# Split weights written to DRAM as two parts, and the router table's writes moved to ScalarE's DMA queue

## The chip, the cores and the metric

The kernel runs on one NeuronCore of a Trainium2 chip. The metric is device time in microseconds (us) of one launch. The kernel before took 3912.41 us (median of three runs, 3896.12 to 3922.23). TensorE (PE) does the matrix products, VectorE (DVE) and ScalarE (ACT) the elementwise work, GpSimd (POOL) issues the indirect gathers, and SyncE (SP) issues nearly all other transfers. SP and ACT each have a DMA queue of their own (q1 and q10 in the profile), POOL's is q0; all three are served by the same 16 DMA engines.

## What is computed

One layer of a hybrid encoder over 1024 prompt tokens and 8 x 16 sample tokens (9 blocks of 128 tokens, width 1024): a combined projection, chunk-band attention, an RG-LRU branch, a gated merge, then PEER (8 heads that each pick 16 of 16384 single-neuron experts).

```python
proj = jnp.einsum('btd,dc->btc', xn, w_in)             # 7 x 1024 columns
q, k, v, x_r, g_branch, gate_a, gate_r = jnp.split(proj, SPLITS, axis=-1)
merged = sigmoid(gate_a) * (o_attn @ w_ba) + sigmoid(gate_r) * (o_lru @ w_bl)
x = x + merged @ w_o
# PEER: s1, s2 = (xt @ wq) . keys; top_k; e_idx; g = softmax(top_s)
act = gelu(einsum('thkd,td->thk', expert_u[e_idx], xt))
out = einsum('thkd,thk->td', expert_v[e_idx], g * act)
```

## The kernel before

Blocks are worked in three groups of three: (0, 1, 8), (2, 3, 4), (5, 6, 7). For each group `mixer` runs five stages: LRU projections, gates and `w_bl`, attention (`w_in` columns for q, k, v and the gates), `w_ba` and `w_o`, and the `wq` projections with the scores. Every group needs the same 96 weight tiles of [128, 8, 128] f32 (512 KB): 56 of `w_in`, 8 each of `w_bl`, `w_ba` and `w_o`, 16 of `wq`. One tile is one projection: 24 matmuls over 384 columns, because each f32 weight w is split into a rounded part hi and a rest lo = w - hi, and `mm3` (L170 to L172) takes the three products hi·hi, hi·lo and lo·hi.

`load_split` makes the two parts. In group 0 it loads `raw` (L149, pool tag "raw", 4 buffers), casts it to hi on ACT (L136), subtracts on DVE (L137), and writes lo to DRAM (L165) for later. In groups 1 and 2 it loads `raw` again, casts it on ACT (L158) and loads lo from DRAM (L159). hi and lo stand in tags "hi" and "lo" of two buffers each, every third pair in `g_p` buffers. The "raw" tag is shared: in the `wq` stage of groups 0 and 1 the gains and the next group's x rows are loaded into it too.

Beside this, five blocks (`DENSE`) get their PEER output from dense products over all experts in a last stage (`dense`), and four (`GATHER`) by gathering rows. The first gather block is interleaved with groups 1 and 2; the others with `dense`. For `dense`, `build_g` makes a router table `G_d` in DRAM. It works through 20 pieces (5 blocks x 4): DVE makes one-hot tiles, PE multiplies them into PSUM tiles `pg` (L1013, L1014), ACT copies eight of these into one SBUF tile `st` (L1016), and `st` is written to `G_d` (L1018), 2 MB in runs of 256 bytes. `st` has one buffer, so the first copy of the next piece must wait until that write has landed. `fill`, `beat` and `tick` spread the pieces over the stages of groups 1 and 2; eight pieces fall into group 1, twelve into group 2.

PSUM tiles of the projections, `pg`, transposes and attention outputs share four buffers (tag "pp"); scores have two (tag "S"). Each engine takes its instructions strictly in the order that the scheduler wrote down; so does SP with its transfers.

Of the kernel before, what the change touches and what calls it, by code (L numbers as in the profile page):

```python
# [10 lines left out]
F32 = mybir.dt.float32  # L11
# [28 lines left out]
RAW_BUFS = 4  # L40
# [19 lines left out]
GCH = 2  # L60
# [5 lines left out]
def r32(ap):  # L66
    return ap.bitcast(F32R)
# [3 lines left out]
def kernel(ctx, tc, a):  # L71
    nc = tc.nc
    V, S, P, T = nc.vector, nc.scalar, nc.gpsimd, nc.tensor

    const = ctx.enter_context(tc.tile_pool(name="const", bufs=1))
    w_p = ctx.enter_context(tc.tile_pool(name="w", bufs=2))
# [5 lines left out]
    dr_p = ctx.enter_context(tc.tile_pool(name="dr", bufs=1, space=bass.MemoryType.DRAM))  # L82
# [52 lines left out]
    def split(hi, lo, src):  # L135
        S.copy(r32(hi), src)  # L136
        ins = V.tensor_tensor(r32(lo), src, hi, op=ALU.subtract)  # L137
        if phase[0] < 3:
            mark("V", ins)

    nw = [0]
    phase = [0, 0]

    lo_d = {}

    def load_split(src, hi=None, lo=None, shape=(128, KT, 128), raw=None, key=None):
        if raw is None:
            raw = w_p.tile(list(shape), F32, name="raw", tag="raw", bufs=RAW_BUFS)
            nc.sync.dma_start(raw, src)  # L149
        if hi is None and phase[0] in THIRD and nw[0] % 3 == 2:  # L150
            hi = g_p.tile(list(shape), F32, name="hi", tag="g3")
            lo = g_p.tile(list(shape), F32, name="lo", tag="g4")
        elif hi is None:
            hi = w_p.tile(list(shape), F32, name="hi", tag="hi")
            lo = w_p.tile(list(shape), F32, name="lo", tag="lo")
        nw[0] += 1
        if key in lo_d:
            S.copy(r32(hi), raw)  # L158
            nc.sync.dma_start(lo, lo_d[key])  # L159
            return hi, lo  # L160
        split(hi, lo, raw)
        if phase[0] == 0 and key:

            lo_d[key] = dr_p.tile(list(shape), F32, name="lo_%s%d" % key)
            nc.sync.dma_start(lo_d[key], lo)  # L165
        return hi, lo

    def mm3(out, l, r, first, last):
# [5 lines left out]
    def proj(src, x, Tn):  # L174

        hi, lo = load_split(a[src[0]][src[1]], key=src)
        ps = ps_p.tile([128, Tn], F32, name="pp", tag="pp")
        for k in range(KT):
            mm3(ps, (hi[:, k, :], lo[:, k, :]), (x[:, 0, k, 0:Tn], x[:, 1, k, 0:Tn]), k == 0, k == KT - 1)
        return ps  # L180
# [571 lines left out]
    def make_tables(b):  # L752
        if b in pending:
            pending.pop(b)()

    def table_parts(tab):
        h = tab.bitcast(F16)
        return h[:, 0:128], h[:, 128:256], tab[:, 128:192].bitcast(BF16), h[:, 384:512], h[:, 512:640]
# [213 lines left out]
    G_d = dr_p.tile([128, 128 // GCH, NCH, GCH, 32], F32, name="G_d")  # L972

    def build_g(gp, b):

        n0 = 4 * DENSE.index(b)
        st = {}

        def part(c, tb):
            def go():  # L980
                if c == 0 and tb == 0:
                    make_tables(b)
                    st["t"] = gp["st"].tile([128, 320], F32, name="tab")
                    nc.sync.dma_start(st["t"], tab_d[b])
                if tb == 0:
                    st["s"] = gp["st"].tile([128, 128, 32], F32, name="st")
                i1, i2, pw, hi, lo = table_parts(st["t"])
                sg = st["s"]
                t = c * 32 + tb * OH_T

                def row(x):
                    return x[:, t:t + OH_T].rearrange("p (g t) -> p g t", t=2).unsqueeze(2).to_broadcast(
                        [128, OH_T // 2, 128, 2])

                ow = gp["oh"].tile([128, OH_T // 2, 128, 2], BF16, name="ow")
                oh = gp["oh"].tile([128, OH_T // 2, 128, 2], F16, name="oh1")
                ol = gp["oh"].tile([128, OH_T // 2, 128, 2], F16, name="oh2")
                V.tensor_tensor(ow, gp["iota"], row(i2), op=ALU.is_equal)
                V.tensor_tensor(ow, ow, row(pw), op=ALU.mult)
                V.tensor_tensor(oh, gp["iota"], row(i1), op=ALU.is_equal)  # L1000
                V.tensor_tensor(ol, oh, row(lo), op=ALU.mult)
                V.tensor_tensor(oh, oh, row(hi), op=ALU.mult)
                later.append(lambda: products(c, tb, ow, oh, ol, sg))
                if len(later) > 1:
                    later.popleft()()
            return go

        def products(c, tb, ow, oh, ol, sg):
            for j0 in range(0, OH_T, 4):
                pg = ps_p.tile([128, 4, 128], F32, name="pg", tag="pp")  # L1010
                for j in range(4):
                    g, e = divmod(j0 + j, 2)
                    T.matmul(pg[:, j, :], ow[:, g, :, e], oh[:, g, :, e], start=True, stop=False)  # L1013
                    T.matmul(pg[:, j, :], ow[:, g, :, e], ol[:, g, :, e], start=False, stop=True)  # L1014
                t = tb * OH_T + j0
                S.activation(sg[:, :, t:t + 4].rearrange("p i t -> p t i"), pg, ACTF.Copy, scale=2.0 ** -13)  # L1016
            if tb == 32 // OH_T - 1:
                nc.sync.dma_start(G_d[:, :, n0 + c], sg.rearrange("p (a i) t -> p a i t", i=GCH))  # L1018

        later = deque()  # L1020
        return [part(c, tb) for c in range(4) for tb in range(32 // OH_T)] + [lambda: later.popleft()()]

    def dense(dp):
# [13 lines left out]
        def u_phase(e):  # L1037
            tick(2)
            hi, lo = load_split(a["peer_ut"][e], raw=u0 if e == 0 else None)
            wh = dp["w"].tile([128, Td], F32, name="wh")  # L1040
            wl = dp["w"].tile([128, Td], F32, name="wl")
            w = dp["w"].tile([128, Td], F32, name="wf", bufs=1)
            for m in range(0, Td, Td // 2):
                c1 = slice(m, m + Td // 2)
                ps = ps_p.tile([128, Td // 2], F32, name="pp", tag="pp")
                for k in range(KT):
                    mm3(ps, (hi[:, k, :], lo[:, k, :]), (xt2[:, 0, k, c1], xt2[:, 1, k, c1]), k == 0, k == KT - 1)
                S.activation(w[:, c1], ps, ACTF.Gelu_apprx_tanh)  # L1048
            w3 = w.rearrange("p (c t) -> p c t", t=32)
            V.tensor_tensor(w3, w3, router(e), op=ALU.mult)  # L1050
            split(wh, wl, w)
            return wh, wl

        def load_v(e):
            vh = dp["v"].tile([128, D], F32, name="vh")
            vl = dp["v"].tile([128, D], F32, name="vl")
            return load_split(a["peer_v"][e], vh, vl, (128, D))
# [254 lines left out]
```

## Time and profile before

| What | Value |
|---|---|
| median of 3 runs | 3912.41 us |
| the profiled execution's own time | 3894.32 us |
| its span in the trace | 3892.5 us |
| PE busy | 3629.8 us (93%) |
| DVE busy | 3049.4 us (78%) |
| ACT busy | 1624.7 us (42%) |
| DMA, mean of the span | 310 GB/s |
| group 0 | 0 to 620 us |
| groups 1 and 2 | 620 to 2055 us |
| dense stage | 2055 to 3892 us |

The page gives, for each engine, its busy time and share. A share over the whole span hides the stages, so the rows below are cut by stage. "Idle before <-" in a row names what ended the wait of that instruction, and a chain piece is a stretch of the path that ended last, followed back from the end.

### The profile page before, as it was taken

The page shows a single profiled execution, that of the slowest core. Times are in us where ns is not written, and L with a number is a line of the kernel's source. Part 1 is how long each engine was busy: PE and PEld are TensorE (multiplying, and loading weights), DVE is VectorE, ACT ScalarE, POOL GpSimd, SP SyncE. Part 2 cuts the span into 40 slices and gives each one's busy share as a digit, 9 for nine tenths or more (in the row PEclk, how much of TensorE's full clock was granted, in tenths as well). Part 3 has the DMA queues.
Part 4 walks back from the last instruction along what each step waited for, and adds up shares of the span by engine and source line. Part 5 has one row for each costly group of instructions (what it writes and reads, how often), then busy time and mean ns, then how long its engine had stood idle before and what let it go on. Part 6 is the DMA issues. An engine that isn't in the chain of part 4 may idle for free.

```text
span 3892.5 us, 59562 instructions
## 1 busy us (share of the span) xinstructions
PE 3629.8 (93%) x21775; PEld 3258.9 (84%) x21775; DVE 3049.4 (78%) x6332; ACT 1624.7 (42%) x2699; POOL 1429.2 (37%) x1094
## 2 busy tenths in 40 slices
PE   8998899899988889988788989999999999999998
PEld 7877799877778887777778878999999999999997
DVE  8433357968766588987669999998888998888997
ACT  7554346656644664666443222222222222222222
POOL 0000000123212012322210666665675665775662
PEclk9999999999999999999889999999999999999999
DMA  7778887888999889899996999898998998998995
GB/s 256 252 247 300 287 295 276 301 315 281 284 358 349 300 299 315 298 290 284 334 337 216 345 326 342 320 347 332 359 339 310 346 347 326 336 349 324 342 343 206
DMA packets 558423, 1208.05 MB, mean 310 GB/s; under 512 B 205361, under 2 KB 281521, under 8 KB 558129
## 3 DMA queue, kind: packets, MB, share of 16 engines
q1 hardware_dynamic: 380560, 638.23, 47.3%
q0 software_dynamic: 147456, 536.94, 38.4%
q10 hardware_dynamic: 30112, 29.09, 2.2%
q8 instruction: 170, 2.79, 0.3%
q14 instruction: 125, 1.02, 0.1%
HBM read 1066.15 MB, written 137.94 MB: 309 GB/s over the span
## 4 chain that ended last, share of the span: by engine, by line
PE 61%; DVE 13%; DMA 10%; ACT 6%; issue 3%; POOL 0%; ACTq 0%; SPq 0%; DVEq 0%; POOLq 0%
PE S L1085 19%; PE pp L170 12%; PE pp L171 12%; PE pp L172 12%; DMA G_d<-st 4%; DVE row L942 3%; PE S L529 2%; ACT st L1016 2%; DMA row<-peer_u,ei 1%; PE pt L458 1%; PE pp L543 1%; ACT hi L158 1%; DVE x L963 1%; DMA lo<-lo_w_in 1%; DVE lo L137 1%
## 5 line engine op out<-in xcount | busy, mean ns | idle before, releaser
L915 POOL DMA_INDIRECT row<-peer_u,ei x512 | 715.2, 1397 | 1172.0 <-DVE row L942 508.6
L915 POOL DMA_INDIRECT row<-peer_v,ei x512 | 687.8, 1343 | 793.4 <-DVE x L963 543.0
L963 DVE SCALAR_TENSOR_TENSOR x<-row,q,x 128x1024 f32<-128x1024 f32 x512 | 655.0, 1279 | 21.3 <-DMA row<-peer_v,ei 12.5
L170 PE MATMUL pp<-xd,hi 128*128 128x320 f32 x2048 | 635.9, 310 | 16.4 <-ACT wf L1048 12.8
L942 DVE SCALAR_TENSOR_TENSOR row<-row,xt 128x1024 f32<-128x1024 f32 x512 | 613.2, 1218 | 42.7 <-DMA row<-peer_u,ei 41.1
L172 PE MATMUL pp<-xd,lo 128*128 128x320 f32 x2048 | 634.3, 310 | 4.5 <-DVE lo L137 4.5
L171 PE MATMUL pp<-xd,hi 128*128 128x320 f32 x2048 | 634.7, 310 | 0.0
L170 PE MATMUL pp<-xn,hi 128*128 128x384 f32 x1344 | 480.2, 358 | 13.9 <-ACT hi L158 6.9
L171 PE MATMUL pp<-xn,hi 128*128 128x384 f32 x1344 | 463.2, 345 | 0.5 <-DVE xn L137 0.5
L172 PE MATMUL pp<-xn,lo 128*128 128x384 f32 x1344 | 461.1, 344 | 0.9 <-DMA lo<-lo_w_in 0.9
L136 ACT CAST hi<-raw 128x1024 fp32r<-128x1024 f32 x223 | 234.0, 1050 | 447.0 <-PE pp L171 329.6
L170 PEld LDWEIGHTS pp<-xd,hi 128*128 128x128 f32 x2048 | 386.8, 189 | 26.0 <-ACT wf L1048 15.6
L137 DVE TENSOR_TENSOR lo<-raw,hi 128x1024 fp32r<-128x1024 f32 x223 | 272.3, 1222 | 171.1 <-ACT hi L136 151.0
L1085 PE MATMUL S<-vh,wh 128*128 128x512 f32 x1280 | 397.2, 392 | 5.2 <-DVE acc L1093 3.5
L1085 PE MATMUL S<-vl,wh 128*128 128x512 f32 x1280 | 396.0, 390 | 1.7 <-DVE vl L137 1.7
L1085 PE MATMUL S<-vh,wl 128*128 128x512 f32 x1280 | 390.1, 394 | 5.9 <-DVE wl L137 5.9
L171 PEld LDWEIGHTS pp<-xd,hi 128*128 128x128 f32 x2048 | 386.7, 189 | 7.1
L172 PEld LDWEIGHTS pp<-xd,lo 128*128 128x128 f32 x2048 | 386.6, 189 | 6.6 <-DVE lo L137 4.8
L158 ACT CAST hi<-raw 128x1024 fp32r<-128x1024 f32 x192 | 200.5, 1047 | 316.3 <-PE pp L171 215.8
L1048 ACT ACTIVATE wf<-pp 128x320 f32<-128x320 f32 x256 | 106.7, 434 | 524.7 <-PE pp L172 316.8
L170 PEld LDWEIGHTS pp<-xn,hi 128*128 128x128 f32 x1344 | 261.7, 195 | 38.3 <-ACT hi L158 9.7
L1085 PEld LDWEIGHTS S<-vh,wl 128*128 128x128 f32 x1280 | 242.2, 190 | 58.3 <-DVE wl L137 7.8
(296 smaller groups left out, 6824.7 us busy)
## 6 DMA issues: line engine op xcount, KB each, us to landing
raw<-w_in SPq DMA_DIRECT2D x168, 512.0 KB
raw<-peer_v SPq DMA_DIRECT2D x128, 512.0 KB
raw<-peer_ut SPq DMA_DIRECT2D x127, 512.0 KB
lo<-lo_w_in SPq DMA_DIRECT2D x112, 512.0 KB
G_d<-st SPq DMA_DIRECT2D x20, 2048.0 KB
gt<-G_d SPq DMA_DIRECT2D x64, 640.0 KB
lo_w_in<-lo SPq DMA_DIRECT2D x56, 512.0 KB
raw<-wq SPq DMA_DIRECT2D x48, 512.0 KB
```

The lines of the kernel that those rows point to most:

```text
L136: S.copy(r32(hi), src)
L137: ins = V.tensor_tensor(r32(lo), src, hi, op=ALU.subtract)
L158: S.copy(r32(hi), raw)
L170: T.matmul(out, r32(lh), r32(rh), start=first, stop=False)
L171: T.matmul(out, r32(lh), r32(rl), start=False, stop=False)
L172: T.matmul(out, r32(ll), r32(rh), start=False, stop=last)
L529: T.matmul(s[:, m, 0:nh], st["q"][r0:r0 + 64, i * 128:(i + 1) * 128], kf[r0:r0 + 64, ko + m * nh:ko + (m + 1) * nh], start=True, stop=True)
L915: P.indirect_dma_start(out=t, out_offset=None, in_=table, in_offset=bass.IndirectOffsetOnAxis(ap=ei[:, j:j + 1], axis=0))
L942: V.scalar_tensor_tensor(u, u, 1.0, xt, op0=ALU.mult, op1=ALU.mult, accum_out=hh[:, j:j + 1])
L963: V.scalar_tensor_tensor(x2, v, q[:, j:j + 1], x2, op0=ALU.mult, op1=ALU.add)
L1048: S.activation(w[:, c1], ps, ACTF.Gelu_apprx_tanh)
L1085: T.matmul(po[:, m, :], r32(l[:, c1]), r32(r[:, m * 512:m * 512 + 512]), start=(n == 0 and q == 0 and (c == 0 or not held)), stop=(n == EC ...
```

## The change

Two things are changed. In group 0 the kernel writes hi as well as lo to DRAM (two transfers of 512 KB per tile, on SP's queue). In groups 1 and 2 it loads both parts and casts nothing: the raw load becomes the load of hi, and the ACT cast L158 is gone. The tiles change their tags in these groups: hi takes the four "raw" buffers and lo alternates between tags "lo" and "hi", four buffers in all. Second, the write of `st` to `G_d` is issued by ACT on its own queue in place of SP.

```diff
     def load_split(src, hi=None, lo=None, shape=(128, KT, 128), raw=None, key=None):
+        if key in lo_d:
+            nw[0] += 1
+            hi = w_p.tile(list(shape), F32, name="hi", tag="raw", bufs=RAW_BUFS)
+            lo = w_p.tile(list(shape), F32, name="lo", tag=("hi", "lo")[nw[0] % 2])
+            for t, d in zip((hi, lo), lo_d[key]):
+                nc.sync.dma_start(t, d)
+            return hi, lo
...
-        if key in lo_d:
-            S.copy(r32(hi), raw)
-            nc.sync.dma_start(lo, lo_d[key])
-            return hi, lo
         split(hi, lo, raw)
         if phase[0] == 0 and key:
-            lo_d[key] = dr_p.tile(list(shape), F32, name="lo_%s%d" % key)
-            nc.sync.dma_start(lo_d[key], lo)
+            lo_d[key] = [dr_p.tile(list(shape), F32, name="%s_%s%d" % (n, *key)) for n in ("hi", "lo")]
+            for t, d in zip((hi, lo), lo_d[key]):
+                nc.sync.dma_start(d, t)
...
-                nc.sync.dma_start(G_d[:, :, n0 + c], sg.rearrange("p (a i) t -> p a i t", i=GCH))
+                nc.scalar.dma_start(G_d[:, :, n0 + c], sg.rearrange("p (a i) t -> p a i t", i=GCH))
```

The scheduler writes a new order from it. Lines of the changed kernel lie five higher from L170 on. In group 0, SP's queue holds this before, near the start (cv and ck are the sample attention's cached values and keys):

```order
L165 DMA lo_w_in32_455<-lo_452 128x1024
L149 DMA raw_685<-w_in 128x1024
L165 DMA lo_w_in27_508<-lo_505 128x1024
L149 DMA raw_738<-w_in 128x1024
L165 DMA lo_w_in33_560<-lo_557 128x1024
```

and this in the changed kernel:

```order
L170 DMA hi_w_in32_461<-hi_457 128x1024
L170 DMA lo_w_in32_462<-lo_458 128x1024
L157 DMA raw_699<-w_in 128x1024
L170 DMA hi_w_in27_516<-hi_512 128x1024
L170 DMA lo_w_in27_517<-lo_513 128x1024
L157 DMA raw_754<-w_in 128x1024
L170 DMA hi_w_in33_570<-hi_566 128x1024
L170 DMA lo_w_in33_571<-lo_567 128x1024
```

One write per tile became two; everything behind them on SP moves back by one transfer per projection.

In the `wq` stage of group 2, ACT's order after the last copy of the second-last piece is, before (so is the score tile copied out, s_d its place in DRAM, pq a projection copied out of PSUM):

```order
L1016 ACTIVATE st_20313<-pg_20796 128x4x128
L729 COPY so_20883<-S_20876 128x768
L730 DMA s_d2_112<-so_20883 128x768
L158 CAST hi_20964<-raw_20962 128x1024
L719 COPY pq_20810<-pp_20752 128x384
L158 CAST hi_21050<-raw_21048 128x1024
L719 COPY pq_20874<-pp_20818 128x384
```

and in the changed kernel:

```order
L1021 ACTIVATE st_20143<-pg_20614 128x4x128
L1023 DMA G_d_135<-st_20143 8192x1x64
L734 COPY so_20699<-S_20692 128x768
L735 DMA s_d2_112<-so_20699 128x768
L724 COPY pq_20690<-pp_20634 128x384
L734 COPY so_20845<-S_20838 128x768
L735 DMA s_d2_112<-so_20845 128x768
L724 COPY pq_20774<-pp_20718 128x384
```

The casts are gone, and the write of the router piece stands two rows ahead of another transfer of ACT's own. Over the 20 pieces, ACT's next own transfer other than a router piece comes 1, 2, 2, 3, 3, 4, 5, 6, 9 and 13 rows behind in ten cases; in the other ten the next piece's write comes first, or 29 or more rows lie between.

In the `wq` stage of group 1, SP's order in the changed kernel is this (x and gain are the next group's rows and gain, in the same four "raw" buffers as hi):

```order
L153 DMA lo_12620<-lo_wq5_5932 128x1024
L153 DMA hi_12619<-hi_wq5_5931 128x1024
L153 DMA lo_12722<-lo_wq6_6047 128x1024
L223 DMA x_12698<-x 128x1024
L153 DMA lo_12784<-lo_wq7_6084 128x1024
L719 DMA keys_12555<-keysT 128x256
L230 DMA gain_12700<-norm_mix 128x1024
L153 DMA lo_12864<-lo_wq8_6177 128x1024
L719 DMA keys_12719<-keysT 128x256
L153 DMA hi_12721<-hi_wq6_6046 128x1024
```

Here hi of tile 6 comes after lo of tile 8: two of the "raw" buffers were given to x and gain first.

## Rows read from the trace of the kernel before

**Rows 1.** The page, part 4: the whole chain that ended last, by line.

```profile
PE S L1085 19%; PE pp L170 12%; PE pp L171 12%; PE pp L172 12%; DMA G_d<-st 4%; DVE row L942 3%; PE S L529 2%; ACT st L1016 2%; DMA row<-peer_u,ei 1%; PE pt L458 1%; PE pp L543 1%; ACT hi L158 1%; DVE x L963 1%; DMA lo<-lo_w_in 1%; DVE lo L137 1%
```

**Rows 2.** Windows by stage: busy time per engine, PE clock, DMA share, GB/s.

```profile
0.00:620.00 620.00, 558.35 (x3814) 503.80 (x3814) 303.43 (x755) 319.78 (x648) 26.27 (x70) 0.96 0.79 272
620.00:980.00 360.00, 339.96 (x1916) 293.55 (x1916) 296.97 (x1066) 219.23 (x390) 69.37 (x64) 0.96 0.83 294
980.00:1330.00 350.00, 302.85 (x1954) 274.57 (x1955) 224.36 (x526) 179.82 (x283) 64.80 (x56) 0.93 0.97 328
1330.00:1640.00 310.00, 285.83 (x1636) 249.24 (x1635) 268.30 (x927) 186.06 (x328) 66.75 (x63) 0.96 0.88 307
1640.00:2055.00 415.00, 349.10 (x2458) 306.49 (x2458) 310.89 (x603) 229.85 (x364) 99.56 (x73) 0.93 0.96 308
2500.00:3892.00 1392.00, 1381.68 (x7742) 1259.33 (x7740) 1216.14 (x1393) 373.19 (x526) 866.19 (x602) 1.00 0.90 329
```

**Rows 3.** Waits of PE, 620 to 2055 us: total, times, longest.

```profile
PE pp L170 <- ACT hi L158: 32.0, 22, 5.9
PE pg L1013 <- ACT st L1016: 20.7, 12, 5.5
...
PE pp L170 <- ACT st L1016: 17.0, 15, 9.3
PE pg L1013 <- ACT pq L719: 14.6, 6, 7.2
PE pt L458 <- ACT st L1016: 8.1, 8, 5.8
```

**Rows 4.** Chain in order of time: start, length, what.

```profile
980.73 16.21 DMA G_d<-st
...
1026.86 17.52 DMA lo<-lo_w_in
...
2008.20 19.37 DMA G_d<-st
```

**Rows 5.** Groups of ACT's instructions: busy, mean ns, idle before and what ended it.

```profile
L158 ACT CAST hi<-raw 128x1024 fp32r<-128x1024 f32 x192 | 200.5, 1047 | 316.3 <-PE pp L171 215.8 <-issue 79.9 <-DMA raw<-w_in 6.9
L1016 ACT ACTIVATE st<-pg 128x512 f32<-128x512 f32 x160 | 160.2, 1106 | 46.3 <-DMA G_d<-st 31.8 <-PE pg L1014 13.0 <-issue 0.5
```

**Rows 6.** Timeline of SP from 1960 us: start, length of the issue.

```profile
1962.15 0.53 SPq L1018 DMA_DIRECT2D G_d<-st  x1
1964.84 15.81 SPq L159 DMA_DIRECT2D lo<-lo_wq  x1
```

**Rows 7.** Timeline of ACT and PE beside it.

```profile
1964.32 0.33 ACTq L730 DMA_DIRECT2D s_d<-so  x1
...
1983.02 0.48 ACT L719 COPY pq<-pp 128x384 f32<-128x384 f32 x1 [10.76 <-DMA G_d<-st]
...
1983.55 0.26 PE L1013 MATMUL pg<-oh,ow 128*128 128x128 f16 x1 [7.21 <-ACT pq L719]
```

**Rows 8.** DMA queues, 1975 to 1977 us: packets, MB, share of 16 engines.

```profile
q1 hardware_dynamic: 2269, 0.58, 127.6%
```

**Rows 9.** DMA queues, 1978 to 1979 us (q1 holds only `G_d` packets).

```profile
q0 software_dynamic: 95, 0.37, 90.7%
q1 hardware_dynamic: 112, 0.03, 12.6%
```

**Rows 10.** DMA queues, 1640 to 2055 us.

```profile
q1 hardware_dynamic: 120430, 81.50, 65.0%
q0 software_dynamic: 10636, 38.72, 25.9%
```

**Rows 11.** Windows of 20 us in group 0 and just behind it.

```profile
480.00:500.00 20.00, 20.00 (x118) 20.00 (x117) 13.58 (x20) 7.83 (x10) 0.00 (x0) 1.00 1.01 383
620.00:640.00 20.00, 19.44 (x114) 18.89 (x115) 14.37 (x64) 8.80 (x11) 0.00 (x0) 1.00 1.02 397
```

**Rows 12.** DMA issues of the page: transfers and KB each.

```profile
G_d<-st SPq DMA_DIRECT2D x20, 2048.0 KB
...
lo_w_in<-lo SPq DMA_DIRECT2D x56, 512.0 KB
```

**Rows 13.** DMA queues, 1249.9 to 1255 us, just behind the issue of a `G_d` write at 1249.85.

```profile
DMA packets 611, 1.99 MB, mean 390 GB/s; under 512 B 76, under 2 KB 76, under 8 KB 611
```

## The prediction

> **What bounds the kernel now.** I read the chain by line first [rows 1]. Most of it is PE, but 4% of 3892.5 us, 156 us, is the writing of the router table to DRAM, `G_d<-st`, and 1% each are the cast L158 and the load of lo. Then the windows by stage [rows 2]. From 2500 us on PE is busy 1381.68 of 1392 us at a clock of 1.00, and the orders of DVE and ACT there are the same before and after but for the stage's first rows, so nothing is to be won or lost there. Whatever happens, happens before 2055 us. Of the four windows from 620 to 2055 us (1435 us) PE is busy 339.96 + 302.85 + 285.83 + 349.10 = 1277.7 us: 157 us idle, 113 of them in the two windows in which router pieces are built (980 to 1330 and 1640 to 2055 us). There the DMA share is 0.97 and 0.96.
>
> The waits of PE in that time [rows 3] say for whom it waits: 32.0 us for the cast L158, and 20.7 + 17.0 + 14.6 + 8.1 = 60.4 us for ACT's copies into `st` or for `pq` copies. The latter are ACT standing in front of a router piece that is still being written: ACT's copies into `st` waited 31.8 us for `G_d<-st` [rows 5], and a `pq` copy another 10.76 us [rows 7]. In the chain by time nine of the 20 writes stand whole, from the first (16.21 us) to the last (19.37 us) [rows 4]. So groups 1 and 2 hang on three things: how soon a 2 MB write lands, what ACT has at its head, and PE.
>
> **The change part by part.**
>
> *Group 0 writes hi too.* 96 transfers of 0.524 MB (the 512 KB of [rows 12]) are 50.3 MB more. Group 0 now moves 272 GB/s x 620 us = 168.6 MB [rows 2]; 219 MB at the 397 GB/s that a 20 us window reaches [rows 11] need 552 us, so on the mean there is room. A dense window has none: at 480 us 383 GB/s flow while 118 matmuls, 4.9 tiles, are worked [rows 11]. 4.9 more writes (2.6 MB on 7.7 MB) at 397 GB/s take 25.8 us in place of 20. I take two such windows, +12 us. Bounds: 0, if the four raw buffers cover it; and +65, if the share cannot rise over the 0.90 of the dense stage: (0.79 x 620 + 50.3 MB / 397 GB/s) / 0.90 = (490 + 127) / 0.90 = 685 us.
>
> *The casts go.* 192 x 1047 ns = 200.5 us of ACT [rows 5]. ACT is busy only 56% of 620 to 2055 us (219.23 + 179.82 + 186.06 + 229.85 of 1435 us), so what counts is what PE waits for: 32.0 us [rows 3]. Not all of that is won. In the `wq` stage of group 1, hi now needs a "raw" buffer that x and the gain hold, and the order shows hi of tile 6 behind lo of tile 8; there the wait for the cast becomes a wait for a load. I take -20 us, between 0 and -32.
>
> *SP is no longer held by the 2 MB write.* Behind a `G_d` write the next issue on SP takes 15.81 us in place of about 0.3 [rows 6], and meanwhile no weights are fetched. In the chain this shows as a load of lo of 17.52 us [rows 4]; all loads of `lo_w_in` on it are 1%, 39 us [rows 1]. lo now has four buffers in place of two or three, so its loads come earlier anyway. -15 us, about one such piece; between 0 and -39.
>
> *The write itself lands later.* This is the term that decides. The table's packets are 256 bytes, those of weights and gathers 4 KB. With nothing beside it the write moves 0.58 MB in 2 us, 290 GB/s [rows 8]; beside the gather queue it gets 0.03 MB in a microsecond in which the gather gets 0.37 [rows 9]. Until now the weights could not do this to it, since they stood behind it in the same queue. The Trainium skill ("DMA: Bandwidth & Descriptors", Queues, rings and completion order) says that each DMA engine takes turns between the queues packet by packet; by that rule a 4 KB packet is served for each 256-byte one, and the trace agrees (0.37 to 0.03 MB). On ACT's queue the weights come past it. From 1640 to 2055 us q1 moves 81.50 MB [rows 10], of which 12 writes of 2.1 MB are 25, so 56 MB / 415 us = 136 GB/s are other transfers. In the 17.5 us that a write takes now, that is 2.4 MB, and at 397 GB/s 6 us more. Against that, the write no longer queues behind loads: 5 us after one issue only 76 of its packets had started [rows 13]; I take 2 us off. +4 us for each of the nine writes on the chain: +36 us. Bounds: -27 (three us won nine times), and +120 (6 us for all 20).
>
> *ACT may stand at its own next transfer.* What held SP for 15.81 us was the queue, not the DMA engines: ACT's own transfers went out in 0.33 us in that time [rows 7]. With the write on ACT's queue, ACT's next transfer is held in the same way, and everything behind it on ACT: projections not copied out, scores not normalized. The price stands in the trace: one hold of ACT of 10.76 us cost PE 7.21 us [rows 7]. In the changed order five of the 20 writes have another ACT transfer within three rows, five more within 13. I take five at 7.2 us, less one that is paid already: +29 us. Bounds: 0 and 10 x 7.2 = +72.
>
> Sum: +12 - 20 - 15 + 36 + 29 = +42 us on the profiled execution's 3894.3 us: 3936. The median of the runs lies 18 us above that execution, so for the median 3954; I say 3955 us.
>
> **Rivals.**
>
> *ACT gains more, and the write is not pushed aside (faster).* Loads of weights are only on their way while buffers are free; with four pairs fetched ahead q1 may be empty when the write starts. ACT idles 316.3 us with a cast at its head [rows 5], and whatever stood behind it waited too, so more than the 32 us may come free: 32 + 30 (half of the 60.4) + 15 - 12 = -65 us, 3847. For it: nearly all of PE's waits are for ACT. Against: the DMA share of 0.96 in exactly these windows. It decides if the write lands within some 17 us and ACT's next transfer still goes out in under a microsecond.
>
> *Gain and loss cancel (no change).* ACT's relief pays for the later write, and the chain moves from the cast to the router piece: 3912 within 1%. The Trainium skill has a rule to this effect ("DMA: Bandwidth & Descriptors", Issuing engines are not separate DMA queues): transfers from all engines interleave on the same 16 DMA engines, and issuing from another engine only saves the issuer's time, usually little. By that the move is worth nothing, and the edits of the weights, +12 - 20, would give 3904. The trace speaks against "little" (15.81 us), not against the rest.
>
> *Every piece becomes bound by its write (much slower).* If the weights push all 20 writes back by 6 us (+120) and group 0 fills its DMA share as well, some +140 us, 4050.
>
> **How the numbers follow.** Chances: the forecast 0.33, much slower 0.10, no change 0.28, faster 0.29. About 1%, 39 us, is what a measurement of this kernel tells from no change. So faster by over 1% 0.29, within 1% 0.28, slower by over 1% 0.43. The forecast's own range is 3925 to 4000; since cases of both signs carry weight, the range reaches into the faster rival and to the edge of the much slower one: 3845 to 4035.
>
> **What would show it.** Group 0 ending later than 620 us by 0 to 30 us shows the first term. No L158 and PE waits for `hi` loads in group 1's `wq` stage show the second. The chain pieces `G_d<-st` say most: 20 to 25 us each, where they are 16 to 20 now, or gone; with them ACT's waits on `G_d`, over 100 us where they are 31.8. ACT issues of 5 us and more right behind a router write show the hold; if all are at 0.3 us, that term is wrong. If q1 still shows an issue held behind a write it does not carry, SP was held by something other than its queue. Dense must keep its 1837 us from 2055 us to the end.

## The result and the profile after

The changed kernel takes 4014.38 us (median; 4009.39 to 4020.77), the kernel before 3904.73 us on the same chip: a ratio of 1.0277, 95% interval 1.0253 to 1.0302. It is slower, by 110 us. The time lies inside the forecast range (3845 to 4035), on the side that held most of the chance (slower, 0.43), but the loss is more than twice the 42 us of the sum.

First the busy times of the whole execution, from the page (us, share of the span, instructions):

```profile
PE 3640.9 (91%) x21775; PEld 3271.9 (82%) x21775; DVE 3053.0 (76%) x6332; ACT 1447.9 (36%) x2507; POOL 1416.8 (35%) x1094
```

PE does the same work in almost the same busy time (3640.9 us, before 3629.8), and its span is 121.1 us longer (4013.6 against 3892.5). So 110 of the 121 us are idle time of PE, not slower matmuls. ACT's busy time fell by 177 us (1624.7 to 1447.9), most of the 200.5 us of the casts [rows 5], and the kernel is slower even so.

Where the 121 us lie is read from the start of the last projection matmul of each group and of the first dense matmul (us):

| | end of group 0 | of group 1 | of group 2 | dense begins | span |
|---|---|---|---|---|---|
| before | 623.8 | 1303.2 | 2048.6 | 2055.8 | 3892.5 |
| after | 653.3 | 1357.4 | 2159.2 | 2182.2 | 4013.6 |
| lost in this stage | +29.5 | +24.7 | +56.4 | +15.8 | -5.3 |

The windows by stage of the changed kernel, in the columns of [rows 2] (busy time of PE, PEld, DVE, ACT, POOL; clock; DMA share; GB/s):

```profile
0.00:620.00 620.00, 540.71 (x3665) 479.69 (x3666) 293.07 (x715) 308.17 (x631) 24.73 (x70) 0.95 0.93 337
980.00:1330.00 350.00, 271.56 (x1796) 245.61 (x1795) 218.00 (x482) 127.84 (x226) 61.69 (x55) 0.86 0.87 290
1640.00:2055.00 415.00, 323.73 (x2226) 277.61 (x2226) 291.90 (x562) 177.87 (x320) 91.25 (x75) 0.87 0.84 270
```

The two windows in which router pieces are built lost 31 and 25 us of PE's busy time against [rows 2], and the DMA engines did less there, not more: a share of 0.87 and 0.84 where it was 0.97 and 0.96. (The windows are the same times; in its work the changed kernel is 17 us behind at the first of these stretches and 110 us at the end of the second.) In group 0 it is the other way about: 0.93 in place of 0.79.

The waits of PE from 620 to 2170 us (in total, times, longest):

```profile
PE pp L175 <- ACT st L1021: 70.0, 11, 17.0
PE S L534 <- ACT p L447: 33.4, 13, 5.8
PE S L732 <- ACT pq L724: 28.7, 8, 14.1
PE pt L463 <- ACT st L1021: 20.8, 4, 10.9
PE tr L699 <- ACT x L704: 19.2, 2, 9.9
PE pg L1018 <- ACT st L1021: 16.5, 4, 8.6
...
PE pp L175 <- DMA hi<-hi_w_in: 9.2, 4, 3.5
PE pp L175 <- DMA hi<-hi_wq: 6.0, 3, 2.9
```

The 32.0 us for the cast [rows 3] are gone; in their place PE waits 15.2 us for loads of hi. The waits for copies into `st` grew from 20.7 + 17.0 + 8.1 = 45.8 us to 70.0 + 20.8 + 16.5 = 107.3 us, and PE now waits 28.7 us for `pq` at the scores and 19.2 us for `x`, copies that stood on ACT behind something held. What ACT and SP waited for in the same time (first ACT's waits, then SP's):

```profile
ACT st L1021 <- DMA G_d<-st: 105.4, 12, 13.3
```

```profile
SPq L153 <- DMA G_d<-st: 82.1, 7, 16.6
...
SPq L688 <- DMA G_d<-st: 16.2, 1, 16.2
```

ACT waits 105.4 us for the write of the table to land (31.8 before, [rows 5]). SP waits for it as well, 122 us in ten waits, although SP no longer carries it and its transfers at these lines don't touch `G_d`: the program gives the transfers of SP and ACT their completion semaphores from one set of eight (in the trace, semaphores 100 and 102 to 108 tell of the landing of SP's 1453 transfers and of ACT's 158 alike), so a load of SP waits until the write that had its semaphore last has landed. The chain in order of time (start, length, what), which in this trace reaches back only to 1741 us, shows six of the writes:

```profile
1741.69 20.51 DMA G_d<-st
...
1856.78 14.97 DMA G_d<-st
1883.70 21.94 DMA G_d<-st
1933.46 25.06 DMA G_d<-st
1978.02 28.67 DMA G_d<-st
2025.90 24.93 DMA G_d<-st
2070.05 13.45 ACTq L705
...
2163.53 10.86 ACTq L735
```

They last 15 to 29 us, five of them over 20, where the nine of before lasted 16 to 20 (the first and the last of them in [rows 4]), and the last two rows are issues: ACT stands at transfers of its own. The timeline of ACT shows such a hold whole (start, length, instruction):

```profile
1301.05 0.55 ACTq L1023 DMA_DIRECT2D G_d<-st  x1
1301.69 15.75 ACTq L713 DMA_DIRECT2D xt_d<-sq  x2
1317.48 0.48 ACT L724 COPY pq<-pp 128x384 f32<-128x384 f32 x1 [16.47 <-issue]
```

The write is issued in 0.55 us. The next two issues, for which ACT has no other reason to stand, take 15.75 us, and the `pq` copy behind them starts 16.47 us late. This is the row of SP in [rows 6], moved to ACT. From 620 us on the changed kernel has eight ACT issues of over 3 us, 95 us together, and none on SP; before it was 18 on SP, 197 us, and none on ACT.

Last, the DMA queues in five microseconds inside the write that starts at 1933 us (packets, MB, share of 16 engines):

```profile
q1 hardware_dynamic: 411, 1.29, 63.7%
q0 software_dynamic: 151, 0.54, 26.3%
q10 hardware_dynamic: 753, 0.19, 16.9%
```

The table's queue q10 gets more packets through than the other two together, and a tenth of all bytes: 0.19 of 2.02 MB. At that rate 2.1 MB would take 55 us; this write landed in 25, since the other queues don't move as much all the time.

### The profile page after: what moved, and what is told of

The parts are those of the page before. It is cut to its first block, busy times and chain, and to the rows that moved or that the text cites. A ratio compares the mean times of both kernels' runs of the same rounds, so it can differ in the third digit from the quotient of the medians.

```text
span 4013.6 us, 59536 instructions
## 1 busy us (share of the span) xinstructions
PE 3640.9 (91%) x21775; PEld 3271.9 (82%) x21775; DVE 3053.0 (76%) x6332; ACT 1447.9 (36%) x2507; POOL 1416.8 (35%) x1094
## 3 DMA queue, kind: packets, MB, share of 16 engines
q14 instruction: 123, 1.01, 0.1%
## 4 chain that ended last, share of the span: by engine, by line
PE 40%; DVE 8%; DMA 5%; issue 1%; ACT 1%; ACTq 1%; POOL 0%; DVEq 0%; POOLq 0%
PE S L1090 17%; PE pp L175 7%; PE pp L177 7%; PE pp L176 7%; DMA G_d<-st 3%; DVE row L947 2%; DMA row<-peer_u,ei 1%; ACTq L735 1%; DVE lo L137 1%; DVE vl L137 0%; ACT st L1021 0%; DVE acc L1098 0%; DVE x L968 0%; ACTq L705 0%; DVE wf L1055 0%
## 5 line engine op out<-in xcount | busy, mean ns | idle before, releaser
L920 POOL DMA_INDIRECT row<-peer_v,ei x512 | 678.4, 1325 | 872.9 <-DVE x L968 593.6
L968 DVE SCALAR_TENSOR_TENSOR x<-row,q,x 128x1024 f32<-128x1024 f32 x512 | 654.6, 1279 | 20.5 <-DMA row<-peer_v,ei 13.6
L136 ACT CAST hi<-raw 128x1024 fp32r<-128x1024 f32 x223 | 234.0, 1050 | 397.4 <-PE pp L176 318.4
L1090 PEld LDWEIGHTS S<-vl,wh 128*128 128x128 f32 x1280 | 240.4, 188 | 52.9 <-DVE vl L137 1.1
## 6 DMA issues: line engine op xcount, KB each, us to landing
G_d<-st ACTq DMA_DIRECT2D x20, 2048.0 KB, 20.5
```

The lines of the kernel that those rows point to most:

```text
L920: P.indirect_dma_start(out=t, out_offset=None, in_=table, in_offset=bass.IndirectOffsetOnAxis(ap=ei[:, j:j + 1], axis=0))
L968: V.scalar_tensor_tensor(x2, v, q[:, j:j + 1], x2, op0=ALU.mult, op1=ALU.add)
L1090: T.matmul(po[:, m, :], r32(l[:, c1]), r32(r[:, m * 512:m * 512 + 512]), start=(n == 0 and q == 0 and (c == 0 or not held)), stop=(n == EC ...
```

## The experiments

All ratios are to the kernel before, run beside each kernel on the same chip; intervals are 95%. The changed kernel was timed on another occasion than e1 to e4, so differences to it are those of the medians; by the ratios they come out 3 to 9 us smaller (100 in place of 109 us for the queue, 21 in place of 24 for e3, 26 in place of 33 for e4).

### e1 and e2: each half of the change alone

e1 takes the kernel before and changes only the queue of the table's write:

```diff
-                nc.sync.dma_start(G_d[:, :, n0 + c], sg.rearrange("p (a i) t -> p a i t", i=GCH))
+                nc.scalar.dma_start(G_d[:, :, n0 + c], sg.rearrange("p (a i) t -> p a i t", i=GCH))
```

> The kernel before with one edit: the router table's write is issued on ACT's queue; the weights are handled as before. Theory (the write on ACT's queue is overtaken by the 4 KB packets of the weights, and ACT is held behind it): most of the loss outside group 0 is here, so +60 to +100 us on the kernel before (ratio 1.015 to 1.026), the G_d writes take 19 to 25 us from issue to landing, and ACT waits over 80 us on G_d. Rival (the loss is in the handling of the weights; the choice of queue only saves SP's time): within 20 us of the kernel before, or below it.

Measured: 4028.37 us against 3899.04, ratio 1.0339 (1.0311 to 1.0366): +129 us, over the +60 to +100 that were expected. The groups end at 623, 1348 and 2173 us, so group 0 loses nothing and groups 1 and 2 lose 125. PE waits for ACT's copies (of PE's waits, 620 to 2170 us):

```profile
PE pg L1013 <- ACT st L1016: 66.4, 14, 13.9
PE pp L170 <- ACT hi L158: 42.1, 23, 13.4
PE pp L170 <- ACT st L1016: 30.5, 14, 16.4
```

The same lines stood at 20.7, 32.0 and 17.0 us [rows 3]. Even the waits for the cast grew, for the casts stand in ACT's queue behind the held copies. The queue alone makes more than the whole loss, and DVE and POOL work in the same written order as before. The chain of e1, unlike that of the changed kernel, reaches back to the start. Eleven writes of the table stand on it, 254 us together, where before nine stood, 157 us; and ACT's issues are 75 us of it, 4.5 before. Behind each of the eleven it is ACT that goes on, and never SP: SP's waits for the table (72 us here) don't stand on this chain.

e2 takes the changed kernel and puts the write back on SP (the diff the other way round).

> The changed kernel with the router table's write put back on SP's queue; only the handling of the weights is changed. Theory: group 0 ends 25 to 30 us later (653 us in place of 624) because of the hi writes, groups 1 and 2 win 10 to 40 us from the casts that are gone, together -15 to +20 us on the kernel before. Rival (hi in the raw buffers makes PE wait for loads in groups 1 and 2): +60 us or more, with PE waits on loads of hi over 40 us.

Measured: 3905.13 us, ratio 1.0022 (1.0008 to 1.0037): no difference that matters. Group 0 ends at 653.8 us, 30 us late; from there to the end of group 2 (2060.5 us) it is 1406.7 us in place of 1424.8. So writing hi costs 30 us in group 0, and reading both parts gives back 18. Where the 18 come from is not shown: PE waits 34 us for loads of hi where it waited 32.0 us for the cast, 17.7 us of it once in the `wq` stage of group 1. ACT's waits for the table are 51.3 us at its copies into `st` here, with the write on SP's queue, so a part of their growth from 31.8 to 105.4 us comes with the weights and not with the queue. The two halves add up: 30 - 18 on the weights, and 109 us between e2 (3905) and the changed kernel (4014).

### e3: ACT carries the table and nothing else

The transfers that ACT is held at (`x2_d`, `xt_d`, `s_d`, L705, L713 and L735) go to SP:

```diff
-            nc.scalar.dma_start(s_d[gi][h], so)
+            nc.sync.dma_start(s_d[gi][h], so)
```

and likewise for the other two.

> The changed kernel, with ACT's own writes of the wq stage (scores, x2 and xt) issued on SP, so that in the wq stages only the router table stands on ACT's queue. Theory with a hold of ACT behind its own write as a cost: ACT's DMA issues of 5 us and more in the wq stages vanish and 20 to 40 us are won on the changed kernel (3975 to 3995). Rival (the hold is hidden, ACT would wait for the write's landing anyway): within 10 us of the changed kernel.

Measured: 3989.95 us, ratio 1.0222 (1.0199 to 1.0246): 24 us less than the changed kernel. Three ACT issues of over 3 us are left, 27.6 us. But the wait that was taken away came back at another place. Waits of ACT and, below, of SP:

```profile
ACT st L1021 <- DMA G_d<-st: 158.2, 16, 18.2
```

```profile
SPq L153 <- DMA G_d<-st: 87.6, 8, 16.2
SPq L735 <- DMA G_d<-st: 40.4, 3, 17.8
```

ACT, no longer held at its own transfer, now arrives at the next copy into `st` sooner and waits there: 158.2 us in place of 105.4. So taking the hold away is worth 24 us as long as the write lands this late. By the stages it is more: dense begins 38 us earlier than in the changed kernel (2144.7 us), but is 15 us longer (1846 us), in a written order that differs too; why is open.

### e4: one hi write in place of 96

95 of the 96 writes of hi are left out. All reads of hi in groups 1 and 2 go to the one tile that is written, so the products are those of a wrong tile; the number and sizes of the reads stay.

```diff
-            lo_d[key] = [dr_p.tile(list(shape), F32, name="%s_%s%d" % (n, *key)) for n in ("hi", "lo")]
-            for t, d in zip((hi, lo), lo_d[key]):
-                nc.sync.dma_start(d, t)
+            if not one_hi:
+                one_hi.append(dr_p.tile(list(shape), F32, name="one_hi"))
+                nc.sync.dma_start(one_hi[0], hi)
+            lo_d[key] = (one_hi[0], dr_p.tile(list(shape), F32, name="lo_%s%d" % key))
+            nc.sync.dma_start(lo_d[key][1], lo)
```

> The changed kernel, but group 0 writes hi of one weight tile only, and groups 1 and 2 read that one tile as hi for all 96 (so the hi part of their products is that of a wrong tile, with the same sizes and loads); 95 of the 96 hi writes are left out. Theory (group 0 is slowed by the DMA engines, which the hi writes fill): group 0 ends within 5 us of 624 us in place of 653, and 25 to 30 us are won on the changed kernel (3985 to 3990). Rival (group 0 is later for another reason, such as the changed order): under 10 us won.

Measured: 3981.51 us, ratio 1.0210 (1.0187 to 1.0233), 33 us less than the changed kernel; group 0 ends at 628.6 us. Its window from 0 to 620 us:

```profile
0.00:620.00 620.00, 551.96 (x3794) 495.83 (x3795) 301.88 (x753) 318.12 (x646) 25.84 (x70) 0.97 0.78 271
```

With the writes gone, the DMA share is at 0.78 again and PE has 11 us back in this window. The 25 us that group 0 wins are the price of 95 writes; the rest of the 33 us lies in groups 1 and 2 and is not explained. Where group 0 loses is read by following the same matmul in both traces. Up to 240 us the changed kernel is less than 1 us behind; at the end of the attention stage (463 us before, 480 after) it is 17 us behind, through `w_ba` and `w_o` it stays at 18, and the `wq` stage adds the rest. The attention stage from 240 us on, with the same 1779 matmuls (first the changed kernel):

```profile
240.00:480.00 240.00, 194.52 (x1779) 155.41 (x1779) 79.93 (x175) 102.91 (x254) 16.40 (x57) 0.90 0.93 335
```

```profile
240.00:463.00 223.00, 190.11 (x1779) 155.19 (x1779) 76.45 (x173) 100.57 (x248) 16.93 (x57) 0.93 0.85 293
```

Here the DMA engines were at 0.85 before the change, with the caches being loaded; the added writes take it to 0.93, PE idles 45 us in place of 33, and its granted clock, which is one of 1.2 and 2.4 GHz at any time, is at the lower level for a larger part of the stretch (mean 0.90 against 0.93).

### e5 to e8: the table in runs of 16 KB

To see whether the size of the packets makes the cost, `G_d` is laid out so that a piece is written in one run of 16 KB per partition. The short runs (256 bytes) move to the reading side, in dense.

```diff
-    G_d = dr_p.tile([128, 128 // GCH, NCH, GCH, 32], F32, name="G_d")
+    G_d = dr_p.tile([128, NCH, 128, 32], F32, name="G_d")
...
-                nc.scalar.dma_start(G_d[:, :, n0 + c], sg.rearrange("p (a i) t -> p a i t", i=GCH))
+                nc.scalar.dma_start(G_d[:, n0 + c], sg)
...
-            nc.sync.dma_start(gt, G_d[:, k])
+            nc.sync.dma_start(gt, G_d[:, :, k * GCH:(k + 1) * GCH])
```

e5 is the changed kernel with it, e6 the same with the write on SP, e7 the kernel before with it.

> The changed kernel with one thing altered: G_d is laid out as [128, 20, 128, 32], so that each of the 20 writes goes out in runs of 16 KB per partition in place of 256 bytes, still on ACT's queue; the 256-byte runs are now on the reading side, in the dense stage (64 loads of 20 runs per partition). If the cost of the move comes from the small packets (turns with 4 KB packets of the other queue, and a full queue behind many descriptors), a write lands in 6 to 12 us in place of 20.5, ACT's waits on G_d fall from 105 us to under 30, ACT's issues over 3 us (8, 95 us) are gone, and the time falls by 90 to 130 us, to about 3885 to 3925. If the cost comes from two queues as such, or from the bytes moved, the write still lands at about 20 us and the time stays within 25 us of 4014. If the loads of the table in 256-byte runs disturb dense, dense is longer than 1831 us.

> The same long runs with the write on SP's queue (two-part weights as in the changed kernel). Small packets as the cause: SP is no longer held and PE waits less for ACT's copies into st; 20 to 60 us below the two-part weights alone (3905), 3845 to 3885, and about the same as on ACT's queue (within 15 us). Queue as the cause: 3905 within 10 us, and the ACT queue 100 us above it.

> The kernel before with nothing but the long runs of G_d. If what the 256-byte write cost before was SP's hold and its late landing (nine chain pieces of 16 to 20 us, 156 us of the chain), 30 to 70 us are won: 3830 to 3870. If the chain only moves on to PE, ACT's casts and the loads of lo, under 15 us.

Measured: e5 3931.04 us, ratio 1.0092 (1.0063 to 1.0121); e6 3918.67, 1.0052 (1.0034 to 1.0069); e7 3931.65, 1.0078 (1.0051 to 1.0104). The write lands in 11.9, 10.5 and 10.9 us, and the queue's price falls from 109 us to 12. On the mechanism the packets won. On the times, the expectations for all three missed, e5's by 6 us: dense begins at 2008, 2002 and 2025 us, in e6 and e7 54 and 31 us earlier than before, and yet the whole is longer, as dense takes 1911 to 1915 us in place of 1837. In e5 the last dense block is done at 3828 us, and behind it POOL and DVE work on gathered rows until 3920 us. The written order had changed in dense: by expert 112 of 128 it has 869 of the 1024 gather rows there in e7, 931 before. How much of the longer dense is that order, and how much the short reads, these runs don't tell. So they answer for the groups, not for the whole.

e8 adds to e6 that hi is written for 40 of the 96 tiles only (LRU stage, `w_bl`, `w_ba`, `w_o`):

```diff
+            two = key[0] in ("w_bl", "w_ba", "w_o") or key[0] == "w_in" and 24 <= key[1] < 40
```

> Long runs on SP's queue, and hi written in group 0 only for 40 of 96 tiles: those of the LRU stage (16 tiles of w_in), w_bl, w_ba and w_o; the other 56 keep raw, cast and lo. The 30 us that group 0 lost lay in the attention stage (17) and the wq stage (10), so group 0 should end within 8 us of 623 us, while 10 of the 24 us that groups 1 and 2 won stay: 10 us under the kernel before with long runs. If the loss comes with the number of writes wherever they stand, group 0 loses 12 us and the two are equal.

Measured: 3926.61 us, ratio 1.0082 (1.0051 to 1.0112). Group 0 ends at 626 us, as expected, so its loss lies in the stages that were left out here. But groups 1 and 2 take 1371 us, where they take 1342 in e6 and 1390 in e7: dense begins at 2004 us in e8 and at 2002 in e6. What group 0 saves (25 us), the casts of the other 56 tiles take back (29 us).

### e9 to e11: runs of 512 bytes, reads unbroken

`G_d` is laid out by four experts in place of two, which doubles the runs of the write and leaves the reads whole. So that the table takes no more room in SBUF, it is read in two halves of 10 chunks, and DVE multiplies in two instructions. The gathers keep their pace in the written order.

```diff
-GCH = 2
+GCH = 4
...
-            V.tensor_tensor(w3, w3, router(e), op=ALU.mult)
+            for gt, n in router(e):
+                V.tensor_tensor(w3[:, n:n + NCH // 2], w3[:, n:n + NCH // 2], gt, op=ALU.mult)
```

> The changed kernel with runs of 512 bytes in the write of the table in place of 256 (G_d laid out by four experts in place of two) and unbroken reads of 5 KB per partition in dense, each table tile read in two halves of 10 chunks (so DVE multiplies in two instructions). Unlike the 16 KB runs, the written order keeps the pace of the gathers in dense (921 of 1024 gather rows by expert 112, 931 in the changed kernel, 869 with the 16 KB runs), so the whole time can be compared. Packets as the cause: half as many, so the landing falls from 20.5 us to about 15, ACT's waits on G_d from 105 to about 60 us, and the time to between 3900 and 3960. Two queues as the cause: 4014 within 20 us.

> The same with the write on SP's queue. Packets as the cause: the gap between ACT's and SP's queue falls from 109 us (4014 against 3905) to 20 to 60 us; this one 3860 to 3895.

> The kernel before with the 512-byte runs alone. SP held for 8 us in place of 16 and the write landing sooner: groups 1 and 2 win 15 to 30 us, 3870 to 3890; if dense loses by the two halves, its length is over 1845 us.

Measured: e9 (ACT's queue) 3985.63 us, ratio 1.0211 (1.0177 to 1.0244); e10 (SP's queue) 3884.66, 0.9966 (0.9948 to 0.9984); e11 (the kernel before) 3905.77, 1.0012 (1.0001 to 1.0022). e9 missed what the packet theory gave: the queue's price is still 101 us. e11 missed its 3870 to 3890 as well: SP's issues of over 3 us fall from 197 to 116 us, yet group 0 ends 7 us later than before and groups 1 and 2 take 10 us more, in an order that differs; why is open. The write lands in 14.3 us on SP, but in 19.6 on ACT's queue, and ACT waits longer than in the changed kernel. In e9, ACT's waits, and the queues in five microseconds inside a write (1843 to 1848 us):

```profile
ACT st L1021 <- DMA G_d<-st: 121.8, 13, 15.2
```

```profile
q1 hardware_dynamic: 289, 0.72, 43.8%
q0 software_dynamic: 166, 0.59, 32.7%
q10 hardware_dynamic: 781, 0.40, 26.4%
```

Why so little is won is read from the packets of all 20 writes, counted from the first to the last packet of each. In the microseconds in which the other two queues move 0.35 MB or more (103 of 342 in the changed kernel, 83 of 310 in e9), q10 gets 88 packets through beside 66 of q1 and 44 of q0; in e9 it is 70 beside 66 and 39. So the doubled size gives q10 0.036 in place of 0.022 MB in such a microsecond, still less than a tenth of the whole, and the loads go past it either way: while the 20 writes are under way, q1 moves 41.4 MB in the changed kernel and 41.2 MB in e9, q0 29 MB in both. With the write on SP's queue (e2), q1 moves only 5.5 MB beside the table's own packets. The longest write of each, from issue to landing (first the changed kernel, 1978.0 to 2006.7 us, then e9, 1960.3 to 1986.1 us):

```profile
q1 hardware_dynamic: 1250, 4.53, 39.6%
q10 hardware_dynamic: 8208, 2.10, 32.2%
```

```profile
q1 hardware_dynamic: 1264, 4.57, 45.1%
...
q10 hardware_dynamic: 4112, 2.10, 26.8%
```

### e12 to e14: the same order, 16 KB runs

e12 is e9 with the write in runs of 16 KB and the reads in dense in runs of 512 bytes:

```diff
-            nc.sync.dma_start(gt, G_d[:, k // 2, n:n + NCH // 2])
+            nc.sync.dma_start(gt, G_d[:, n:n + NCH // 2, k // 2 * GCH:k // 2 * GCH + GCH])
```

with the layout of e5. The written order of all engines is the same as in e9, row for row. e13 is the same from e10, e14 from e11.

> The kernel of e9 (write on ACT's queue, tables read in two halves) with the write in runs of 16 KB per partition in place of 512 bytes, and the reads in dense in runs of 512 bytes in place of 5 KB. The written order of all engines is that of e9, row for row, so nothing but the size of the table's packets differs before the dense stage. Packets as the cause: landing 11 to 13 us in place of 19.6, ACT's waits on G_d 20 to 40 us in place of 122, no issue of ACT over 3 us, and 3850 to 3890: 95 to 135 us below e9. Another queue as such as the cause: 3985 within 25 us.

> The same change of runs from e10 (write on SP's queue), again in the same written order. Packets as the cause: within 20 us of the same on ACT's queue, 3845 to 3875, which is faster than the kernel before by 1% or about. If the write on SP's queue was bound by its bytes, 3885 as in e10.

> The same runs in the kernel before (one-part weights): 3855 to 3885. The difference to e13 is what the two-part weights are worth once the table's write no longer disturbs: 0 to 25 us in their favour by the stages of e6 and e7 (group 0 loses 23, groups 1 and 2 win 48).

Measured: e12 3871.23 us, ratio 0.9921 (0.9904 to 0.9939); e13 3852.93, 0.9874 (0.9857 to 0.9891); e14 3883.89, 0.9953 (0.9934 to 0.9971). The three times lie in their ranges; the 31 us between e14 and e13 lie over the 0 to 25 that were expected. With nothing changed but the runs, the kernel with the write on ACT's queue becomes 114 us faster, and the queue's price is 18 us. In e12, ACT's waits, and the queues inside a write (1930 to 1935 us):

```profile
ACT st L1021 <- DMA G_d<-st: 18.9, 8, 4.7
```

```profile
q10 hardware_dynamic: 202, 1.15, 55.2%
q1 hardware_dynamic: 360, 0.92, 48.5%
q0 software_dynamic: 22, 0.05, 2.7%
```

Now q10 moves more bytes than the other two together. While the 20 writes are under way, q1 moves 8.8 MB and q0 6.8, where it was 41.2 and 29 in e9. No issue of ACT takes over 2 us, and PE's waits for copies into `st` are down to this (waits of PE, 620 to 2140 us):

```profile
PE pp L175 <- ACT st L1021: 15.3, 10, 4.0
PE pt L463 <- ACT st L1021: 6.0, 10, 2.4
```

e13 is the best of all: two-part weights, the write on SP's queue, 16 KB runs, 1.3% under the kernel before, where the changed kernel is 2.8% above it.

The queue's price by the size of the runs (medians, ACT's queue less SP's, two-part weights both times): 109 us at 256 bytes, 101 at 512, 12 and 18 at 16 KB. The whole time also holds dense, which no edit of the queue or the weights touches, so here is the start of dense and its length (us, from the traces):

| | 256 bytes | 512 bytes | 16 KB (e12 to e14) |
|---|---|---|---|
| two parts, ACT's queue: dense begins, lasts | 2182.2, 1831 | 2147.2, 1837 | 2014.6, 1859 |
| two parts, SP's queue | 2069.3, 1837 | 2047.1, 1836 | 2009.7, 1843 |
| one part, SP's queue | 2055.8, 1837 | 2073.6, 1839 | 2020.4, 1863 |

Up to dense the queue's price is 113, 100 and 5 us. With the short reads dense takes 7 to 24 us longer, in the same written order. And of the 31 us between e14 and e13 only 11 lie before dense; the other 20 are dense itself. Up to dense the two-part weights cost 13 us at 256 bytes and win 26 and 11 us at the others, each pair in different written orders.

Two things were not tried: a second `st` buffer, so that ACT need not wait for the landing, and a semaphore of its own for the table's write, so that SP need not wait for it. How the price of 109 us divides between ACT's waits (105 us in the changed kernel) and SP's (122 us) is therefore not measured; that no SP wait follows a write of the table on the chains of e1 and e9, which reach back to the start, speaks for ACT's.

## Why the prediction was half right

Its mechanism held: groups 1 and 2 hang on how soon the table's write lands, and on ACT's queue it lands later and holds ACT. The sum failed in the sizes of two terms, group 0 and above all the landing, and in one gain of which no run shows that it came. The three terms of the queue, -15 + 36 + 29 = +50 us, measure +113 us up to dense (e2 to the changed kernel), and +134 in e1.

**Group 0 writes hi too (+12).** Measured +30 us in the changed kernel and in e2, and e4 has 25 of it back in group 0 (33 in the whole). Inside the bounds of 0 to +65, but mis-sized. The step that failed is the choice of the dense window. I took 20 us at 480 us with a share of 1.01, and two such windows. That window lost nothing: the matmul that started at 480.2 us starts 17.9 us later in the changed kernel, and so does the one that started at 496.8. 17 us are lost before it, in the attention stage, a stretch of 223 us at 0.85, and some 10 behind it in the `wq` stage; both were hidden in a mean of 0.79 over 0 to 620 us. I had warned that a share over the span hides the stages, and then read group 0 as one stage.

**The casts go (-20).** The number was right: from the end of group 0 to that of group 2, e2 wins 18 us. The reason was right in part: hi of group 1's `wq` stage came late, as I had read from the order, and in e2 the waits for hi (34 us) are as long as those for the cast were (32.0 us). So the 18 us are not those waits, and that the number fits may be luck. With the write out of the way (e14 to e13) the same stretch wins 48 us, and group 0 loses 35.

**SP not held (-15).** SP's long issues are gone, 18 before and none after, but SP now waits at its own transfers for `G_d<-st` (122 us, 82.1 of them at L153). I had listed what would show that SP was held by "something other than its queue"; what it met was another: a semaphore shared with ACT's transfers. On e1's chain the loads of lo are 31 us where they were 54, so some of the gain may have come; by itself it was not measured. Where a transfer moves to another queue, the waits of the old queue's owner have to be read again.

**The write lands later (+36).** The size by write was right: over all 20 writes the median time from the issue to the end of the last packet went from 16.2 to 20.2 us. The reason held in its larger part, for q1 moved 41.4 MB meanwhile, 2.1 MB a write, where I had taken 2.4 (and nearly all of it new: 5.0 MB before); the 2 us that I took off didn't come (the first packet starts 3.8 us after the issue, 3.3 before). What failed is what I multiplied it by: the nine writes that stood whole in the chain of before. A write that lands later brings others into the chain, and those that stand there already are the ones that more goes past: e1's chain has eleven of 23.1 us in the mean where there were nine of 17.5, so 254 us in place of 157, +97. That is inside my bounds of -27 to +120, near the upper one. This is the term that made the forecast less than half of what was measured.

**ACT stands at its own next transfer (+29).** About right: 24 us by e3 in the whole, 38 up to dense, and eight long issues where I had taken five. A third of the 38 lies between the last projection of group 2 and dense, where 15.8 us are lost in the changed kernel and 2 in e3 (9.5 us from the one to the other, 7.2 before): the chain stands at ACT's issue there (L735, 10.86 us).

**Dense** kept its length (1831 us from its first matmul to the end, 1837 before).

Up to dense, which begins 126 us later: 30 (hi) - 18 (casts) + 38 (hold, by e3) + 75 (landing and SP's waits, the remainder of 113) = 125 us. The remainder is not measured by itself; the forecast had +36 - 15 = +21 for it.

Two readings were off without weight: ACT is busy 57% of 620 to 2055 us, not 56, and the loads of `lo_w_in` on the chain are 30 us, not 39 (1% was rounded).

Of the rivals, "much slower" (all twenty writes 6 us later, +120) came closer than the forecast in the time (4050, 0.10), but not for its reason: the writes are 4 us later, and eleven of twenty stand on the chain of e1. Faster needed the write to land in 17 us and ACT's next issue in under a microsecond, and neither was so. "No change" rested on the rule in the Trainium skill ("DMA: Bandwidth & Descriptors", Issuing engines are not separate DMA queues). The first half of it is what the traces show: the transfers interleave on the same DMA engines. The second half, that another issuer only saves issue time and that this is usually small, is contradicted by e1: +129 us for one word changed. The other rule of that page (Queues, rings and completion order: each DMA engine takes turns between its queues, packet by packet) agrees with the microseconds of e9 and the changed kernel in which the other queues move 0.35 MB or more: q10 gets 70 and 88 packets through (as the profile counts them), q1 66 in both and q0 39 and 44, and the bytes go with the size of the packets.

## What to carry to other kernels

Here SP's queue protected a transfer of small packets from the transfers that were issued behind it in the same queue (5.5 MB went past 20 writes); on a queue of its own it shared by packets, and 41 MB went past. So before moving a transfer, look at its runs: with 16 KB runs on the side that something waits for, and short ones on the side that is fetched ahead, the move costs 18 us in place of 101, and with the write left on SP's queue the layout wins another 32 us (e10 to e13). Doubling the runs to 512 bytes was not enough. And where a write stands in many places of the waits, count its lateness at each place where its buffer is reused, not only at the pieces that are on the chain today.

## What the runs showed of the hardware

While the other queues move little (under 0.02 MB in the microsecond), the table's write moves 0.25 MB a microsecond in runs of 256 bytes (changed kernel), 0.28 in runs of 512 (e9) and 0.41 in runs of 16 KB (e12). While they move 0.35 MB or more, it moves 0.022 and 0.036 MB at 256 and 512 bytes, so the loads go past it at either size, and the doubling changes little. The median landing on ACT's queue only went from 20.5 to 19.6 us by the doubling and the price from 109 to 101 us; on SP's queue the landing went from 16.1 to 14.3 us. The hold of the issuing engine behind a transfer of many small packets follows the transfer from queue to queue (issues of over 3 us from 620 us on: 197 us on SP before, 95 us on ACT after, none on either in groups 1 and 2 of e12), and gets shorter with fewer packets (with the write on SP's queue, 18 issues and 215 us in e2, 17 and 138 us in e10 with half the packets).
